# Retention layer of a hybrid decoder: chunks flow across heads, and PSUM banks are chosen by the expected end of their last use

## Chip, cores, metric

The kernel runs on the 8 cores of one Trainium2 chip. Each core has one prompt sequence of 2048 tokens (plus 16 meta tokens) and 16 of the 128 sample tokens; the cores share no data. The metric is device time of the slowest core, in microseconds. Some executions on all 8 cores are slower, with a lower granted clock on the cores of one die (one of the kernel before took 2028 us, with 0.83 on cores 0 to 3 and 0.96 on cores 4 to 7). They are called slow here; only the others, the fast ones, are compared.

## The reference, cut

Two layers: a pooling mixer with a SwiGLU feed-forward, then a retention mixer with a SwiGLU feed-forward. The change is in the retention mixer: four heads, keys of 256 and values of 512, in chunks of 128 tokens.

```python
def ret_chunk(q, k, v, s0, log_g):
    scores = jnp.einsum('bihd,bjhd->bhij', q, k) * dmask
    o = jnp.einsum('bhij,bjhe->bihe', scores, v)
    o = o + jnp.einsum('bihd,bhde->bihe', q, s0) * cross[None, :, :, None]
    s_new = gamma ** c * s0 + jnp.einsum('bjhd,bjhe->bhde', k * kdec, v)
    return o, s_new
# retention_mix: proj = xn @ w_in  -> q, k, v, gate; rotary on q and k; scan of ret_chunk over chunks;
# per-head group norm of o; (silu(gate) * o) @ w_out
```

The 2048 tokens are run as two halves of 1024. So there are two retention stages, each with 4 heads of 8 chunks, and between them lie the feed-forward layers and the sample tokens' states (here "the middle").

## The kernel before

One Python program emits the instructions of all engines, in an order that is fixed at build time. To choose it, the program keeps a clock of its own: every instruction has a modelled cost, and each engine a time at which it is free. Projections are emitted by plain loops. Work of the recurrence is in generators ("side tasks"), which are polled between blocks of a projection and go on when the modelled TensorE time has come to what they wait for. `drain` emits nothing else until a task is finished. A bank is a PSUM buffer of 128 x 512 numbers that a group of matmuls writes and another engine reads; five or six of them go round.

```python
        def bank(hold=False):
            sd.poll()
            ...
            while True:                      # round robin over the banks that nobody holds
                b = ring['b'][ring['i'] % len(ring['b'])]
                ring['i'] += 1
                if b not in held:
                    break
            if hold:
                held.append(b)
            return b
        ...
        def gate_gen(po, n, h, eps_ap, gdst, gsrc, after=None, guard=None, freed=None):
            yield after
            s, x = gn_stats(po, n, eps_ap)   # statistics: VectorE, GpSimd
            yield x
            o = on[onx[0] % 3]
            ...
            x = act(o[0:n, :], po, ACT.Identity, scale=s[0:n, 8:9], bias=s[0:n, 9:10])   # "on"
            if freed is not None:
                freed()                      # the bank may be given out again
            yield x
            yield from room(3)
            pt = bank(True)
            ...                              # four transposes of "on", four affine steps "af", product with the gate
        ...
        def a_gen(hf, h, gap):               # scores and decayed keys of a head, chunk by chunk
            ...
            for t in range(8):
                ps = bank()
                ...
                tt(PMt[:, t, :], ps[:, 0:128], causal, ALU.mult)
                act(KD[:, t, :], ptb, ACT.Copy, scale=float(gam[h] ** (-128.0 * t)))
                yield gap

        def b_gen(hf, h, gap):               # the recurrence
            q = Q[h % 2]
            So = FB[2]
            if hf == 0:
                ...
            else:
                load(So[:], sscr[h], ('fb', 2), ins=[('scr%d' % h)])
                acopy(psS[:], So[:].rearrange("p (c e) -> p c e", c=2))
            xs = acopy(Sbf[0][:], psS[:])
            ...
            for t in range(8):
                ...                          # 5 matmuls, cast of the state to Sbf, one gate_gen as its tail
            while any(x in sd.tasks for x in tails):
                yield 0.3

        def ret(hf, hh, qk_blocks, g_blocks, o_blocks, exit_fn):
            ...
            for h in range(4):
                qk_proj(hf, h, qk_blocks, h == 0)
                if h < 3:
                    g_proj(hf, h, g_blocks)
                sd.drain(bent)               # recurrence of the head before, with all its tails
                aent = sd.add(a_gen(hf, h, 1.3))
                v_proj(hf, h)
                sd.drain(aent)
                bent = sd.add(b_gen(hf, h, (1.5, 2.5, 2.5, 1.0)[h]))
                if h == 3:
                    g_proj(hf, h, g_blocks)
                if h:
                    ...
                    o_proj(hf, h - 1, hh, o_blocks)
            sd.drain(bent)
            ...
            o_proj(hf, 3, hh, o_blocks, exit_fn)
```

Scores `PMt`, decayed keys `KD`, values `V` and keys `K` have one buffer each; queries and gates have two. That is why the value projection of a head has to wait for the recurrence of the head before.

Of the kernel before, what the change touches and what calls it, by code (L numbers as in the profile page):

```python
# [54 lines left out]
class Prog:  # L55
# [109 lines left out]
    def _clock(self, o, ins, outs, cost, nbytes):  # L165

        t = self.free[o.eng]
        for d in o.deps:
            if d.is_dma or d.eng != o.eng:
                t = max(t, d.t + 0.12)  # L170
        if o.is_dma:
            busy = 1.1 if o.eng == 'pool' else 0.08
            self.free[o.eng] = t + busy
            self.dma_free = max(self.dma_free, t + busy) + nbytes / 330e3
            o.t = max(self.dma_free, t + busy + 2.0)
            return
        if cost is None:
            n = outs[0].free_size() if outs else 0
            if o.eng == 'act':
                cost = 0.22 + n / 1400.0  # L180
            elif o.eng == 'dve':
                cost = 0.08 + n / 960.0
            else:
                cost = 0.2 + n * 0.0024
        o.t = t + cost
        self.free[o.eng] = o.t
# [101 lines left out]
class Side:  # L288
# [33 lines left out]
    def drain(self, ent):  # L322
        while ent in self.tasks:
            nxt = min(e[0] for e in self.tasks)
            self.p.free['pe'] = max(self.p.free['pe'], nxt)
            self.poll()
# [26 lines left out]
def build_program():  # L353
# [40 lines left out]
    with st:  # L394
# [126 lines left out]
        held = []  # L521

        def room(k):
            while sum(b not in held for b in ring['b']) < k:
                yield 0.3

        def bank(hold=False):
            sd.poll()
            assert sum(b not in held for b in ring['b']) > 0
            while True:  # L530
                b = ring['b'][ring['i'] % len(ring['b'])]
                ring['i'] += 1
                if b not in held:
                    break
            if hold:
                held.append(b)
            return b
# [19 lines left out]
        def plan_ret():  # L557
            for h in range(4):
                wl.append(w_qk[h, 0])
                wl.append(w_qk[h, 1])  # L560
                for w in ((w_g, w_v) if h < 3 else (w_v, w_g)):
                    wl.append(w[h, 0])
                    wl.append(w[h, 1])
                if h:
                    wl.append(w_o[h - 1, 0])
                    wl.append(w_o[h - 1, 1])
            wl.append(w_o[3, 0])
            wl.append(w_o[3, 1])
# [120 lines left out]
        def pool_a(s0, T, special, ahead, pumps=()):  # L689
# [6 lines left out]
            def front(g):  # L696
                bd = B_BAND + g * 143
                DF = DFA[g % 2]
                for j in range(2):
                    c = 2 * g + j  # L700
                    pd = bank()
                    cc = slice(c * 128, (c + 1) * 128)
# [8 lines left out]
                    if special:  # L711
# [8 lines left out]
                        ts(DF[j][:, n + 16:n + 32], pp[:, 16:32], gcol, None, ALU.mult, ALU.bypass)  # L720
                    x = act(DF[j][:, 0:n], pd[:, 0:n], ACT.Copy, scale=gcol)
                pbs = []
                for m in range(2):
# [161 lines left out]
        stx = [0]  # L885
        gdone = {}
        afb = [False]

# [37 lines left out]
        def a_gen(hf, h, gap):  # L926
            q = Q[h % 2]
            yield rope[0]
            if hf == 0:
                pt = bank()  # L930
                ptb = pt[:].bitcast(BF16)[:, 0:256]
                for c in range(2):
                    tr(ptb[0:32, c * 128:(c + 1) * 128], K[:, c, 1024:1056], ident)
                acopy(KD[0:32, 8, :], ptb[0:32, :])
                copy(qS[:, h, :, :], q[:, :, 1024:1040], 'pool')
                copy(kS[:, h, :, :], K[:, :, 1024:1040], 'pool')
                yield gap
            for t in range(8):
                cc = slice(t * 128, (t + 1) * 128)
                ps = bank()  # L940
                for c in range(2):
                    mm(ps[:, 0:128], K[:, c, cc], q[:, c, cc], c == 0, c == 1)
                pt = bank()
                ptb = pt[:].bitcast(BF16)[:, 0:256]
                for c in range(2):
                    tr(ptb[:, c * 128:(c + 1) * 128], K[:, c, cc], ident)
                tt(PMt[:, t, :], ps[:, 0:128], causal, ALU.mult)
                act(KD[:, t, :], ptb, ACT.Copy, scale=float(gam[h] ** (-128.0 * t)))
                yield gap

        def b_gen(hf, h, gap):
            q = Q[h % 2]
            So = FB[2]
            if hf == 0:
                for c in range(2):
# [5 lines left out]
            yield xs  # L961
            tails = []
            for t in range(8):
                cc = slice(t * 128, (t + 1) * 128)
                while len(tails) > 2 and tails[-3] in sd.tasks:
                    yield 0.3
# [9 lines left out]
                else:  # L976
                    act(So[:].rearrange("p (c e) -> p c e", c=2), psS[:], ACT.Copy, scale=float(gam[h] ** 1024.0))
                    store((sscr if hf == 0 else nrp)[h], So[:], ('fb', 2), outs=[('scr%d' % h)] if hf == 0 else [])
                gs = G[h % 2][:, :, cc]
                tails.append(sd.add(gate_gen(psO[:], 128, h, cf[:, C_GE + h:C_GE + h + 1], gs, gs, after=xo,  # L980
                                             guard=lambda t=t: gdone[h] >= (t + 1) * 128, freed=lambda p=psO: held.remove(p))))
                yield xs
                yield gap
            while any(x in sd.tasks for x in tails):
                yield 0.3

# [39 lines left out]
        def v_proj(hf, h):  # L1026
            ws = [wget(), wget()]
            wv = [w[1][:].rearrange("p (k n) -> p k n", k=4) for w in ws]
            for t in ([8] if hf == 0 else []) + list(range(8)):
                n = 32 if t == 8 else 128  # L1030
                pb = bank()
                for k in range(8):
# [3 lines left out]
                if t == 8:  # L1036
                    acopy(vS[32 * h:32 * h + 16, :], pb[0:16, :])
                    store(vscr[:, h, :], vS[32 * h:32 * h + 16, :], 'vscr', outs=[('vscr%d' % h)])
                sd.poll()
# [20 lines left out]
        def o_proj(hf, h, hh, blocks, exit_fn=None):  # L1060
            ws = [wget(), wget()]
            wv = [w[1][:].rearrange("p (e n) -> p e n", e=4) for w in ws]

            def one(m, c0, n):
                pb = bank()
                for e in range(4):
# [129 lines left out]
        def ret(hf, hh, qk_blocks, g_blocks, o_blocks, exit_fn):  # L1196
            bent = None
            ring['b'] = psM + [psU] if hf == 0 else psM
            for h in range(4):
                gdone[h] = 0  # L1200
                qk_proj(hf, h, qk_blocks, h == 0)
                if h < 3:
                    g_proj(hf, h, g_blocks)
                sd.drain(bent)
                aent = sd.add(a_gen(hf, h, 1.3))
                v_proj(hf, h)
                sd.drain(aent)
                bent = sd.add(b_gen(hf, h, (1.5, 2.5, 2.5, 1.0)[h]))
                if h == 3:
                    g_proj(hf, h, g_blocks)  # L1210
                if h:
# [5 lines left out]
                    o_proj(hf, h - 1, hh, o_blocks)  # L1217
            sd.drain(bent)
            if hf == 1:
                copy(G[1][:, :, 1024:1040], gsm[:, 3, :, :], 'pool')  # L1220
            o_proj(hf, 3, hh, o_blocks, exit_fn)
            ring['b'] = psM

        def xload(h, xT, c0, n, k, eng='sp'):
# [190 lines left out]
```

## Time and profile before

| | us |
|---|---|
| device time, median of 3 | 1834.68 (1833.81 to 1837.03) |
| span of the slowest core (core 3) | 1829.8 |
| TensorE busy there | 1648.8, 90% |
| VectorE, ScalarE, GpSimd busy | 753, 695, 302 |

The stages of core 3 in the profile of the kernel before: first retention stage, middle, second retention stage. A stage here goes from its first query and key matmul to the first matmul of what follows, so it is 12 and 34 us wider than the windows that the prediction uses. After the times come length, busy us with instruction counts of PE (TensorE's matmuls), PEld (its weight loads), DVE (VectorE), ACT (ScalarE) and POOL (GpSimd), then TensorE's granted clock, the DMA share and GB/s. In the lists of waits further down, a line names the tile that waits, the engine and tile that it waits for, and then total us, number of waits and the longest.

```profile
325.18:667.63 342.45, 301.00 (x1817) 162.71 (x1814) 160.38 (x340) 170.92 (x336) 95.53 (x160) 0.97 0.36 73
667.63:1226.04 558.41, 515.88 (x2638) 237.21 (x2638) 234.68 (x328) 241.79 (x365) 55.91 (x95) 0.95 0.81 212
1226.04:1573.27 347.23, 295.48 (x1768) 161.82 (x1765) 169.20 (x375) 167.72 (x319) 95.25 (x152) 0.95 0.31 61
```

Length minus the first busy number is TensorE's idle time: 41 us, 43 us and 52 us. The busy number also holds the cost of a low clock, because a matmul at a lower clock is busy for longer (the prediction shows a group of eight that takes 3.59 us after a wait and 1.90 us elsewhere; the granted clock was 0.50 from 576 to 580 us and 1.00 from 360 to 364).

### The profile page before, as it was taken

The page shows a single profiled execution, that of the slowest core. Times are in us where ns is not written, and L with a number is a line of the kernel's source. Part 1 is how long each engine was busy: PE and PEld are TensorE (multiplying, and loading weights), DVE is VectorE, ACT ScalarE, POOL GpSimd, SP SyncE. Part 2 cuts the span into 40 slices and gives each one's busy share as a digit, 9 for nine tenths or more (in the row PEclk, how much of TensorE's full clock was granted, in tenths as well). Part 3 has the DMA queues.
Part 4 walks back from the last instruction along what each step waited for, and adds up shares of the span by engine and source line. Part 5 has one row for each costly group of instructions (what it writes and reads, how often), then busy time and mean ns, then how long its engine had stood idle before and what let it go on. Part 6 is the DMA issues. An engine that isn't in the chain of part 4 may idle for free.

```text
span 1829.8 us, 28085 instructions; the slowest of 8 cores (1811.3 to 1829.8 us)
## 1 busy us (share of the span) xinstructions
PE 1648.8 (90%) x9925; PEld 919.7 (50%) x9925; DVE 753.0 (41%) x1426; ACT 694.8 (38%) x1263; POOL 301.6 (16%) x505
## 2 busy tenths in 40 slices
PE   4999999898998888978997999999889976999997
PEld 3666666554544443433444444444454533666665
DVE  3532223442644463333346343353544625522224
ACT  3311112155545544433454444432545455310121
POOL 2010000341413111010011000022413312101000
PEclk9899999999998989988998999999999989999998
DMA  7357857623331349688779899772333232245432
GB/s 183 56 91 166 196 119 162 148 43 69 67 60 37 58 108 225 160 200 183 184 185 252 269 260 297 208 171 49 67 70 70 47 81 45 41 71 83 78 55 94
DMA packets 70680, 229.09 MB, mean 125 GB/s; under 512 B 7856, under 2 KB 11120, under 8 KB 70400
## 3 DMA queue, kind: packets, MB, share of 16 engines
q0 software_dynamic: 30224, 103.30, 32.9%
q1 hardware_dynamic: 40320, 124.00, 21.4%
q8 instruction: 83, 1.36, 0.3%
q14 instruction: 53, 0.43, 0.1%
HBM read 254.79 MB, written 62.00 MB: 173 GB/s over the span
## 4 chain that ended last, share of the span: by engine, by line
PE 76%; DVE 7%; DMA 6%; issue 4%; ACT 4%; POOL 2%; SPq 0%; DVEq 0%; POOLq 0%; ACTq 0%
PE pm L474 65%; PE psU L474 5%; PE psS L474 4%; DMA U<-xtok 4%; ACT on L491 2%; DVE xn L507 1%; DVE rot L498 1%; DVE stt L892 1%; ACT af L491 1%; PE pm L482 1%; DMA fb<-sret 1%; DMA U<-gb 1%; POOL U L498 1%; DMA U<-xsp 1%; POOL stt L626 1%
## 5 line engine op out<-in xcount | busy, mean ns | idle before, releaser
L474 PE MATMUL pm<-xn,w 128*128 128x512 bf16 (+7 forms) x4392 | 804.5, 342 | 34.2 <-DVE xn L507 12.9
L474 PEld LDWEIGHTS pm<-xn,w 128*128 128x128 bf16 x4392 | 431.2, 99 | 384.1 <-issue 65.8
L474 PE MATMUL pm<-U,w 128*128 128x512 bf16 (+4 forms) x2203 | 417.7, 346 | 25.1 <-ACT on L491 19.0
L474 PEld LDWEIGHTS pm<-U,w 128*128 128x128 bf16 x2203 | 215.7, 99 | 207.5 <-issue 42.4
L491 ACT ACTIVATE rot<-pm 128x512 bf16<-128x512 f32 (+4 forms) x202 | 104.7, 519 | 438.5 <-PE pm L474 438.5
L498 DVE TENSOR_TENSOR U<-pm,rot 128x512 bf16<-128x512 f32 (+4 forms) x187 | 112.4, 601 | 339.2 <-PE pm L474 331.0
L498 DVE TENSOR_TENSOR hB<-pm,hB 128x347 f32<-128x347 f32 (+2 forms) x161 | 87.1, 551 | 110.2 <-PE pm L474 107.8
L474 PE MATMUL pm<-w,xn 128*128 128x512 bf16 (+1 forms) x448 | 113.4, 399 | 0.0
L498 DVE TENSOR_TENSOR hA<-pm,hA 128x512 f32<-128x512 f32 (+2 forms) x121 | 76.6, 639 | 82.2 <-PE pm L474 82.1
L491 ACT ACTIVATE Sbf<-psS 128x1024 bf16<-128x1024 f32 x56 | 57.3, 1024 | 114.7 <-PE psS L474 114.7
L498 POOL TENSOR_TENSOR U<-rot 128x352 bf16<-128x352 f32 (+2 forms) x96 | 88.8, 946 | 71.9 <-DVE rot L498 71.8
L498 DVE TENSOR_TENSOR rot<-pm,cs_sb 128x352 f32<-128x352 f32 (+2 forms) x170 | 79.3, 512 | 31.0 <-PE pm L474 18.9
L491 ACT ACTIVATE U<-pm 128x256 bf16<-128x256 bf16 (+3 forms) x127 | 58.4, 461 | 84.2 <-PE pm L474 84.0
L491 ACT ACTIVATE af<-pm,cf_sb 128x128 f32<-128x128 bf16 x208 | 78.1, 462 | 21.0 <-PE pm L482 14.0
L498 DVE TENSOR_TENSOR U<-af,U 128x512 bf16<-128x512 f32 x64 | 52.5, 821 | 75.6 <-ACT af L491 75.6
L200 POOL DMA_DIRECT2D w<-w_gu x71 | 40.4, 570 | 257.9 <-PE pm L474 203.9
L491 ACT ACTIVATE U<-pm,cf_sb 128x512 bf16<-128x512 f32 (+1 forms) x72 | 49.0, 686 | 76.7 <-PE pm L474 76.7
L498 DVE TENSOR_TENSOR U<-pm,cb_sb 128x128 bf16<-128x128 f32 x64 | 18.7, 292 | 136.6 <-PE pm L482 101.2
L200 POOL DMA_DIRECT2D w<-w_d x48 | 26.8, 559 | 271.3 <-PE pm L474 230.8
L626 POOL TENSOR_TENSOR stt<-stt,cf_sb 128x1 f32<-128x1 f32 x65 | 39.0, 600 | 172.3 <-DVE stt L502 166.5
L491 ACT ACTIVATE xn<-hB 128x512 bf16<-128x512 f32 (+2 forms) x80 | 42.3, 544 | 66.2 <-DVE hB L498 66.0
L474 PEld LDWEIGHTS pm<-w,xn 128*128 128x128 bf16 (+1 forms) x448 | 42.7, 101 | 45.4 <-issue 8.4
(214 smaller groups left out, 1502.8 us busy)
## 6 DMA issues: line engine op xcount, KB each, us to landing
w<-w_gu POOLq DMA_DIRECT2D x71, 512.0 KB, 7.2
fb<-sret SPq DMA_DIRECT2D x36, 512.0 KB, 7.7
nrs<-fb SPq DMA_DIRECT2D x36, 512.0 KB, 7.2
w<-w_d POOLq DMA_DIRECT2D x48, 352.0 KB, 5.3
hA<-sret SPq DMA_DIRECT2D x28, 512.0 KB, 6.7
nrs<-hA SPq DMA_DIRECT2D x28, 512.0 KB, 5.4
c_gu<-w SPq DMA_DIRECT2D x17, 512.0 KB, 6.6
w<-c_gu POOLq DMA_DIRECT2D x17, 512.0 KB, 9.2
```

Of the source, the lines that this page charges most:

```text
L200: h.dma_start(out=o_ap, in_=i_ap).then_inc(s, 16)
L474: return P.op('pe', lambda h: h.matmul(out, lhsT=lhsT, rhs=rhs, start=start, stop=stop, skip_group_check=skip), ins=[lhsT, rhs], outs=[out ...
L482: return P.op('pe', lambda h: h.transpose(out, in_, idn), ins=[in_, idn], outs=[out], cost=0.056)
L491: return P.op('act', lambda h: h.activation(out=out, in_=in_, func=func, scale=scale, **kw), ins=ins, outs=[out] + ([accum] if accum is no ...
L498: return P.op(eng, lambda h: h.tensor_tensor(out=out, in0=a, in1=b, op=op), ins=[a, b], outs=[out])
L507: return P.op('dve', lambda h: h.scalar_tensor_tensor(out=out, in0=a, scalar=s, in1=b, op0=op0, op1=op1), ins=ins, outs=[out])
L626: return P.op('pool', lambda h: h.tensor_tensor(out=dst, in0=dst, in1=cf[0:n, C_NH:C_NH + k], op=ALU.pow), ins=[dst, cf[0:n, C_NH:C_NH + k ...
L892: P.op('dve', lambda h: h.bn_stats(out=s[0:n, 0:6], in_=po), ins=[po], outs=[s[0:n, 0:6]])
```

## The change

Its intent: the drain between heads goes. Each chunk waits only for the chunk whose buffer it takes, so the recurrence of one head runs on through the projections of the next. A bank is given out by the modelled end of its last use. The modelled costs of ScalarE and VectorE are made a little higher.

```diff
@@ the program's clock
             if o.eng == 'act':
-                cost = 0.22 + n / 1400.0
+                cost = 0.32 + n / 1450.0
             elif o.eng == 'dve':
-                cost = 0.08 + n / 960.0
+                cost = 0.13 + n / 1000.0
@@ banks
+        def idle_since(b):
+            k = P._keys(b[:])[0][0]
+            st = P.segs.get(k)
+            assert st is None or st[0].eng != 'pe' or not st[1]
+            return max(st[0].t if st else 0.0, P.free['pe']), taken.get(k, 0)
+
         def bank(hold=False):
             sd.poll()
-            ... round robin ...
+            b = min((x for x in ring['b'] if x not in held), key=idle_since)
+            ring['i'] += 1
+            taken[P._keys(b[:])[0][0]] = ring['i']
@@ a_gen (the bank of the scores is now held until the mask is applied; so is one in the pooling front)
+                while h and prog['b', h - 1] < t + 1:
+                    yield 0.3
-                ps = bank()
+                yield from room(2)
+                ps = bank(True)
@@ b_gen
+            while prog['v', h] < 1 or prog['a', h] < 1 or h and prog['b', h - 1] < 8:
+                yield 0.3
-                while len(tails) > 2 and tails[-3] in sd.tasks:
+                while len(tl) > 2 and tl[-3] in sd.tasks or prog['v', h] < t + 1 or prog['a', h] < t + 1:
                     yield 0.3
-            while any(x in sd.tasks for x in tails):
-                yield 0.3
@@ v_proj
+                if h:
+                    sd.until(lambda: prog['b', h - 1] > t % 8)
@@ o_proj, before each block
+                for t in range(8):
+                    if t * 128 < c0 + n:
+                        sd.until(lambda: len(tails[h]) > t and tails[h][t] not in sd.tasks)
@@ ret
                 qk_proj(hf, h, qk_blocks, h == 0)
-                if h < 3:
-                    g_proj(hf, h, g_blocks)
-                sd.drain(bent)
                 aent = sd.add(a_gen(hf, h, 1.3))
+                g_proj(hf, h, g_blocks)
+                sd.add(b_gen(hf, h, GAPS[h]))          # GAPS = (2.5, 2.5, 2.5, 1.0)
                 v_proj(hf, h)
                 sd.drain(aent)
-                bent = sd.add(b_gen(hf, h, (1.5, 2.5, 2.5, 1.0)[h]))
-                if h == 3:
-                    g_proj(hf, h, g_blocks)
...
-            sd.drain(bent)
```

Cut: the updates of the counters `prog`, and the weights' order for the last head, which follows the program.

More of the change, by code (lines that the diff above doesn't have):

```diff
@@ L322, in drain, with until @@
     def drain(self, ent):
-        while ent in self.tasks:
+        self.until(lambda: ent not in self.tasks)
+    def until(self, cond):
+        while not cond():
             nxt = min(e[0] for e in self.tasks)
@@ L525, in room @@
                 yield 0.3
+        taken = {}
+        def idle_since(b):
[3 more added lines that the diff above has]
+            return max(st[0].t if st else 0.0, P.free['pe']), taken.get(k, 0)
         def bank(hold=False):
             sd.poll()
-            assert sum(b not in held for b in ring['b']) > 0
-            while True:
-                b = ring['b'][ring['i'] % len(ring['b'])]
-                ring['i'] += 1
-                if b not in held:
-                    break
+            b = min((x for x in ring['b'] if x not in held), key=idle_since)
+            ring['i'] += 1
+            taken[P._keys(b[:])[0][0]] = ring['i']
             if hold:
@@ L560, in plan_ret @@
                 wl.append(w_qk[h, 1])
-                for w in ((w_g, w_v) if h < 3 else (w_v, w_g)):
+                for w in (w_g, w_v):
                     wl.append(w[h, 0])
@@ L700, in front @@
                     c = 2 * g + j
-                    pd = bank()
+                    pd = bank(True)
                     cc = slice(c * 128, (c + 1) * 128)
@@ L721, in front @@
                     x = act(DF[j][:, 0:n], pd[:, 0:n], ACT.Copy, scale=gcol)
+                    held.remove(pd)
                 pbs = []
@@ L886, in build_program @@
         gdone = {}
+        prog = {}
+        tails = {}
         afb = [False]
@@ L928, in a_gen @@
             yield rope[0]
+            while h and prog['b', h - 1] < 1:
+                yield 0.3
             if hf == 0:
@@ L947, in a_gen @@
                 tt(PMt[:, t, :], ps[:, 0:128], causal, ALU.mult)
+                held.remove(ps)
                 act(KD[:, t, :], ptb, ACT.Copy, scale=float(gam[h] ** (-128.0 * t)))
+                prog['a', h] = t + 1
                 yield gap
@@ L953, in b_gen @@
             So = FB[2]
+            while prog['v', h] < 1 or prog['a', h] < 1 or h and prog['b', h - 1] < 8:
+                yield 0.3
             if hf == 0:
@@ L961, in b_gen @@
             yield xs
-            tails = []
+            tl = tails[h] = []
             for t in range(8):
                 cc = slice(t * 128, (t + 1) * 128)
-                while len(tails) > 2 and tails[-3] in sd.tasks:
+                while len(tl) > 2 and tl[-3] in sd.tasks or prog['v', h] < t + 1 or prog['a', h] < t + 1:
                     yield 0.3
@@ L979, in b_gen @@
                 gs = G[h % 2][:, :, cc]
-                tails.append(sd.add(gate_gen(psO[:], 128, h, cf[:, C_GE + h:C_GE + h + 1], gs, gs, after=xo,
+                tl.append(sd.add(gate_gen(psO[:], 128, h, cf[:, C_GE + h:C_GE + h + 1], gs, gs, after=xo,
                                              guard=lambda t=t: gdone[h] >= (t + 1) * 128, freed=lambda p=psO: held.remove(p))))
+                prog['b', h] = t + 1
                 yield xs
                 yield gap
-            while any(x in sd.tasks for x in tails):
-                yield 0.3
         rope = [None]
@@ L1037, in v_proj @@
                     acopy(vS[32 * h:32 * h + 16, :], pb[0:16, :])
+                else:
+                    prog['v', h] = t + 1
+                if t == 8:
                     store(vscr[:, h, :], vS[32 * h:32 * h + 16, :], 'vscr', outs=[('vscr%d' % h)])
@@ L1196, in ret @@
         def ret(hf, hh, qk_blocks, g_blocks, o_blocks, exit_fn):
-            bent = None
             ring['b'] = psM + [psU] if hf == 0 else psM
             for h in range(4):
-                gdone[h] = 0
+                gdone[h] = prog['a', h] = prog['b', h] = prog['v', h] = 0
+            for h in range(4):
                 qk_proj(hf, h, qk_blocks, h == 0)
-                if h < 3:
-                    g_proj(hf, h, g_blocks)
-                sd.drain(bent)
                 aent = sd.add(a_gen(hf, h, 1.3))
+                g_proj(hf, h, g_blocks)
+                sd.add(b_gen(hf, h, GAPS[h]))
                 v_proj(hf, h)
                 sd.drain(aent)
-                bent = sd.add(b_gen(hf, h, (1.5, 2.5, 2.5, 1.0)[h]))
-                if h == 3:
-                    g_proj(hf, h, g_blocks)
                 if h:
@@ L1222, in ret @@
             ring['b'] = psM
+        GAPS = (2.5, 2.5, 2.5, 1.0)
         def xload(h, xT, c0, n, k, eng='sp'):
```

## The prediction

> **What bounds the kernel now.** I read the page first: TensorE is busy for 90% of the span, no other engine above 41%, so time comes only from TensorE's idle time and from a slow clock.
>
> ```profile
> PE 1648.8 (90%) x9925; PEld 919.7 (50%) x9925; DVE 753.0 (41%) x1426; ACT 694.8 (38%) x1263; POOL 301.6 (16%) x505
> ...
> PE   4999999898998888978997999999889976999997
> ...
> PEclk9899999999998989988998999999999989999998
> ```
>
> The idle time is 1829.8 - 1648.8 = 181.0 us. The row of tenths dips in three places: the start, the middle, and the two retention stages. Next I read the busy time by stage, to place the change. The columns are PE, PEld, DVE, ACT, POOL, clock, DMA share, GB/s.
>
> ```profile
> 150.00:200.00 50.00, 50.00 (x337) 32.78 (x336) 14.61 (x28) 2.78 (x6) 5.00 (x10) 1.00 0.75 155
> ...
> 325.00:655.00 330.00, 289.87 (x1734) 157.01 (x1733) 150.20 (x324) 164.06 (x325) 93.52 (x158) 0.96 0.36 72
> ...
> 1243.00:1556.00 313.00, 266.93 (x1573) 143.92 (x1572) 142.16 (x319) 158.10 (x298) 87.03 (x142) 0.97 0.32 63
> ```
>
> A feed-forward stretch is full (50.00 of 50.00 at clock 1.00); nothing can be won there. The two retention stages leave 40.1 and 46.1 us of TensorE idle, 86.2 us together. ScalarE is only half busy in them (164.06 of 330). Third view: TensorE's waits in the first, then in the second retention stage.
>
> ```profile
> PE pm L474 <- ACT on L491: 14.7, 12, 2.5
> PE pm L482 <- ACT on L491: 12.9, 6, 4.4
> PE pm L474 <- DVE xn L507: 4.7, 1, 4.7
> PE pm L474 <- ACT af L491: 3.7, 4, 1.8
> PE psU L474 <- ACT on L491: 2.0, 1, 2.0
> PE psU L474 <- ACT af L491: 1.0, 1, 1.0
> ```
>
> ```profile
> PE pm L482 <- ACT on L491: 23.2, 12, 4.0
> PE pm L474 <- ACT on L491: 15.9, 8, 2.4
> PE pm L474 <- ACT Sbf L491: 2.9, 4, 1.4
> PE psU L474 <- ACT on L491: 1.9, 1, 1.9
> PE psU L482 <- ACT on L491: 1.5, 1, 1.5
> ```
>
> L474 is the matmul helper and L482 the transpose helper; "on" is the group-normalised output of a chunk. So two kinds of waits carry the loss. Kind A: a projection's matmul waits although its data is old. What it waits for is the bank it was given, which ScalarE is still reading (on, af). First stage 14.7 + 3.7 + 2.0 + 1.0 = 21.4; second 15.9 + 1.9 = 17.8; together **39.2 us in 27 waits**. Kind B: the transposes of "on" come before their input is there. 12.9 + 23.2 + 1.5 = **37.6 us in 19 waits**. Kind C, the cast state Sbf: 0.8 + 2.9 = **3.7 us**. The timeline of TensorE shows both of the first two:
>
> ```profile
> 534.86 1.89 PE L474 MATMUL pm<-U,w 128*128 128x512 bf16 x8
> 538.32 1.02 PE L474 MATMUL pm<-U,w 128*128 128x512 bf16 x4 [1.57 <-ACT on L491]
> ```
>
> ```profile
> 568.20 0.59 PE L474 MATMUL psS<-U 128*128 128x512 bf16 x2
> 573.20 0.59 PE L482 MATMUL pm<-cb_sb,on 128*128 128x128 bf16 x4 [4.40 <-ACT on L491]
> 575.63 0.59 PE L482 MATMUL pm<-cb_sb,on 128*128 128x128 bf16 x4 [1.84 <-ACT on L491]
> 576.14 3.59 PE L474 MATMUL pm<-w,xn 128*32 128x512 bf16 x8
> ```
>
> The first is kind A inside the output projection. The second is the drain at the end of a head: the last chunk's normalisation runs alone, and only then does the value projection (576.14) start. It needed nothing of that head but room in the value, score and key buffers.
>
> [...] at 573.20 one transpose holds back a projection whose inputs are ready. [...] after the 4.40 us wait, eight matmuls of 512 columns take 3.59 us; the same group takes 1.90 us at 362.13. [...] The kernel does rotate; kind A shows that a blind rotation meets long holders. [...]
>
> **The change part by part.** No arithmetic is added or removed: the same matmuls, casts and transfers. What moves is the order fixed at build time, by a clock that the program models.
>
> *Bank choice.* Round robin gives way to the bank with the earliest expected end of its last use. The model's ScalarE cost goes from 0.22 + n/1400 to 0.32 + n/1450: 0.59 to 0.67 at 512, 0.95 to 1.03 at 1024, against 0.69 and 1.02 in the trace, so these expectations are good. One gap stays: the model prices the statistics by their 6 outputs, 0.14 us against 0.69 measured, so it thinks "on" ready some 0.6 us early. There are five or six banks, and a chunk holds one or two of them, so another bank is nearly always free earlier. I take 80% of kind A: 0.8 x 39.2 = **31 us**.
>
> *Waits per chunk.* The drain ahead of each value projection goes. Scores of head h run beside its gate projection, its recurrence beside its value projection, the previous head's output projection, and the next head's query and key projections. Would the recurrence be done when the next head needs its buffers? A chunk costs five matmuls of 0.215 = 1.07 us, then the cast 1.02 and its hops, then the gap of 2.5: about 5 us, 40 us for eight. The value projection is 8 x 1.73 = 14 us, the output projection 16 x 0.86 = 14, query and key 14, plus the chunks' own 8.6: about 50 us. So the new waits are met before they are reached. Only the last head cannot hide all: its final chunk's chain (statistics 0.69 + 0.18 + 0.21, GpSimd 0.56 + 0.26, ScalarE 0.78, transposes, four af 1.50, product 0.69, hops) is some 6 us, but the output projection's first block of 8 x 0.86 = 7 us needs only early chunks. I take 80% of kind B: 0.8 x 37.6 = **30 us**; and 70% of C: **2.6 us**.
>
> *Clock.* I compared slow groups after the waits with normal ones. At 426 1.5 us are lost, at 576 2.0, at 648 2.1 (16 matmuls in 5.75 for about 3.6), at 1328 1.7, at 1406 1.5, at 1472 to 1481 2.5, at 1530 1.5: 12.8 us. With the waits of 3 us and more gone, most returns: **10 us**.
>
> *New cost.* In the last head all per-chunk work meets: value copy 0.69, key copy 0.38, Sbf 1.02, on 0.78, af 1.50: 4.4 us of ScalarE per chunk, against 1.73 + 0.43 + 1.07 + 0.22 = 3.5 us of TensorE. I allow 2 us per stage there, 2 per stage for transposes put too early (before, waits of 0.45 to 1.3 us apart from drains), and 1 per stage for the end: **10 us**. Banks held in the pooling front and longer holds of scores cost nothing that I can see.
>
> Sum: 31 + 30 + 2.6 + 10 - 10 = 63.6 us. 1834.7 - 63.6 = **1771 us**, 3.5% less.
>
> **The rivals.** *ScalarE becomes the bound.* The new overlap puts casts, value copies and affine steps in the same 20 us. For it: 4.4 against 3.5 us per chunk. Against: only the last head has the short gap of 1.0; the others start a chunk about every 5 us, and the output projection beside it gives ScalarE nothing. If it holds in every head, 4 us in each of eight heads come back: about 1800 us. *The waits move.* Bank waits become early-transpose waits, as the hidden 0.6 us comes up for each of 64 chunks. For it: seven or so such waits exist already. Against: projection blocks of 0.6 to 1.7 us between polls usually cover it. If half of the chunks pay 0.6: 19 us, so about 1785. *The gain meets something outside.* The middle, with 11.0 us on pooling input, might absorb an earlier start. But its work is placed relative to TensorE's progress, so I expect it to move along whole; 5 us either way.
>
> **Range and chances.** If bank choice and chunk flow recover 95% and the new cost is 4: 37 + 36 + 3 + 12 - 4 = 84, so about 1750. If they recover 55% with half of the clock and 12 lost: 22 + 21 + 2 + 6 - 12 = 39, so about 1796. I give **1748 to 1801**. The 2% line is 1798, near that upper end: faster 0.86, same 0.12, slower 0.02.
>
> **What would show it.** Right: in the retention stages TensorE's idle falls from 86 to about 25 us, "pm L474 <- ACT on" to below 8, no transposes wait over 3 us outside a last head, and the clock there is near 0.99. Wrong: waits on value copies (U from pm) or on score reads appear, ScalarE near 90% in the value projections (first rival); transposes with more waits than 19 and a sum above 20 us (second); or shorter retention stages with a longer middle (third).

## The result, and the profile after

| | before | after |
|---|---|---|
| device time, median of 4 runs each | 1834.24 us | 1752.10 us (1747.89 to 1753.17) |
| ratio of fast runs | | 0.9546 (95%: 0.9526 to 0.9566) |

A ratio is the mean time of one kernel's fast runs over that of the other's fast runs of the same rounds, so it is not quite the ratio of the medians. The change saves 82 us where 63.6 were predicted; 1752 lies in the predicted range, near its lower end. Results are correct.

The page of the kernel after (slowest core: core 1). The matmul helper is now L477, the transpose helper L485.

```profile
PE 1627.1 (93%) x9925; PEld 913.3 (52%) x9925; DVE 749.2 (43%) x1426; ACT 693.7 (40%) x1263; POOL 302.6 (17%) x505
...
PE   4999999999999989897997999999989998999997
...
PEclk7899999999999999998998999999999999999998
```

The instruction counts are the same as before: 9925 matmuls, 1426 on VectorE, 1263 on ScalarE. Only order and banks moved. The same three stages, on core 1:

```profile
323.61:637.08 313.47, 295.90 (x1816) 162.59 (x1814) 163.29 (x346) 171.70 (x337) 97.89 (x160) 0.98 0.41 79
637.08:1182.99 545.91, 508.95 (x2638) 233.65 (x2638) 232.67 (x325) 240.67 (x364) 54.20 (x94) 0.97 0.82 216
1182.99:1499.37 316.38, 288.91 (x1768) 160.76 (x1766) 164.62 (x375) 166.19 (x318) 95.49 (x153) 0.96 0.34 66
```

The retention stages are 29 and 31 us shorter. Their idle time falls from 41 to 18 and from 52 to 27 us, and their busy time by 5 and 7 us at a higher clock (0.97 to 0.98 and 0.95 to 0.96). TensorE's waits in the first, then in the second retention stage after:

```profile
PE psU L477 <- ACT on L494: 5.3, 7, 1.2
PE pm L477 <- DVE U L501: 3.4, 4, 2.0
PE pm L477 <- DVE xn L510: 3.1, 3, 2.1
PE pm L477 <- ACT xn L494: 2.1, 2, 1.8
PE psU L485 <- ACT on L494: 0.6, 1, 0.6
```

```profile
PE pm L477 <- DVE U L501: 6.9, 5, 4.1
PE pm L477 <- ACT U L494: 6.1, 1, 6.1
PE pm L477 <- ACT on L494: 5.5, 5, 1.3
PE pm L477 <- DVE xn L510: 4.0, 7, 2.0
PE pm L485 <- ACT on L494: 3.0, 4, 1.1
```

The long waits of transposes on "on", up to 4.4 us, are gone: none is above 1.1. Bank waits on "on" are left, but none is above 1.3. New are a single wait of 6.1 us on ScalarE's value copy (`U`) and waits on VectorE's `U` of up to 4.1. The experiments come back to both.

### The profile page after: what moved, and what is told of

It reads as the page before. It is cut to its first block, busy times and chain, and to the rows that moved or that the text cites. A ratio compares the mean times of both kernels' runs of the same rounds, so it can differ in the third digit from the quotient of the medians.

```text
span 1751.4 us, 28088 instructions; the slowest of 8 cores (1741.4 to 1751.4 us)
## 1 busy us (share of the span) xinstructions
PE 1627.1 (93%) x9925; PEld 913.3 (52%) x9925; DVE 749.2 (43%) x1426; ACT 693.7 (40%) x1263; POOL 302.6 (17%) x505
## 4 chain that ended last, share of the span: by engine, by line
PE 77%; DMA 8%; DVE 7%; issue 3%; ACT 2%; POOL 2%; SPq 0%; DVEq 0%; POOLq 0%; ACTq 0%
PE pm L477 65%; PE psU L477 6%; DMA U<-xtok 5%; PE psS L477 5%; DVE xn L510 1%; PE pm L485 1%; ACT on L494 1%; DMA nrs<-fb 1%; DVE stt L904 1%; DVE hB L501 1%; DMA fb<-sret 1%; DVE rot L501 1%; DVE hA L501 1%; DMA U<-xsp 1%; POOL stt L635 1%
## 5 line engine op out<-in xcount | busy, mean ns | idle before, releaser
L477 PE MATMUL pm<-xn,w 128*128 128x512 bf16 (+7 forms) x4368 | 798.2, 340 | 19.6 <-DVE hA L510 9.4
L477 PEld LDWEIGHTS pm<-xn,w 128*128 128x128 bf16 x4368 | 426.2, 99 | 357.6 <-issue 42.7
L477 PE MATMUL pm<-U,w 128*128 128x512 bf16 (+4 forms) x2173 | 407.9, 344 | 14.0 <-DVE U L501 7.8
L477 PEld LDWEIGHTS pm<-U,w 128*128 128x128 bf16 x2173 | 211.4, 98 | 190.0 <-issue 22.7
L501 DVE TENSOR_TENSOR hB<-pm,hB 128x346 f32<-128x346 f32 (+2 forms) x154 | 83.4, 552 | 104.1 <-PE pm L477 103.5
L477 PE MATMUL pm<-w,xn 128*128 128x512 bf16 (+1 forms) x480 | 112.7, 383 | 7.1 <-ACT U L494 6.1
L501 POOL TENSOR_TENSOR U<-rot 128x352 bf16<-128x352 f32 (+2 forms) x96 | 90.3, 962 | 58.4 <-DVE rot L501 58.3
L494 ACT ACTIVATE U<-pm 128x256 bf16<-128x256 bf16 (+3 forms) x124 | 54.1, 460 | 73.3 <-PE pm L477 73.1
L635 POOL TENSOR_TENSOR stt<-stt,cf_sb 128x1 f32<-128x1 f32 x65 | 39.2, 604 | 246.2 <-DVE stt L505 246.2
L477 PEld LDWEIGHTS pm<-w,xn 128*128 128x128 bf16 (+1 forms) x480 | 45.5, 98 | 59.9 <-issue 11.2
```

Of the source, the lines that this page charges most:

```text
L477: return P.op('pe', lambda h: h.matmul(out, lhsT=lhsT, rhs=rhs, start=start, stop=stop, skip_group_check=skip), ins=[lhsT, rhs], outs=[out ...
L494: return P.op('act', lambda h: h.activation(out=out, in_=in_, func=func, scale=scale, **kw), ins=ins, outs=[out] + ([accum] if accum is no ...
L501: return P.op(eng, lambda h: h.tensor_tensor(out=out, in0=a, in1=b, op=op), ins=[a, b], outs=[out])
L635: return P.op('pool', lambda h: h.tensor_tensor(out=dst, in0=dst, in1=cf[0:n, C_NH:C_NH + k], op=ALU.pow), ins=[dst, cf[0:n, C_NH:C_NH + k ...
```

## The experiments

Most of what follows is read from two tables. Each number is the mean over all 8 cores of the profiled execution, which is steadier than one core. First the length of the stages, in us. "Start" is all before the first query and key matmul, "end" all after the second retention stage.

| kernel | start | retention 1 | middle | retention 2 | end | ratio to before |
|---|---|---|---|---|---|---|
| before | 321.9 | 343.0 | 551.4 | 347.5 | 256.6 | 1 |
| before, again | 324.0 | 343.1 | 553.0 | 347.5 | 257.0 | |
| costs only | 325.6 | 340.9 | 555.7 | 357.1 | 253.9 | 1.0063 |
| bank choice only | 320.8 | 328.6 | 545.8 | 334.9 | 251.2 | 0.9837 |
| bank choice, costs | 322.5 | 325.6 | 547.2 | 342.8 | 253.0 | 0.9835 |
| flow only | 323.3 | 337.2 | 546.5 | 334.2 | 259.1 | 0.9866 |
| flow, costs | 326.9 | 333.9 | 541.2 | 327.7 | 254.1 | 0.9814 |
| bank choice, flow | 321.9 | 317.5 | 543.8 | 316.8 | 251.8 | 0.9620 |
| after (all three) | 323.4 | 313.3 | 540.0 | 317.8 | 252.5 | 0.9546 |
| after, again | 322.3 | 313.5 | 537.6 | 317.2 | 252.3 | 0.9549 |

Second, TensorE's waits in the two retention stages together. Kind A are matmuls that wait for ScalarE's "on" or "af" to free their bank; kind B are transposes that wait for "on".

| kernel | A, bank waits | B, early transposes | A + B |
|---|---|---|---|
| before | 39.5 | 37.7 | 77.2 |
| costs only | 44.5 | 42.4 | 86.9 |
| bank choice only | 16.3 | 42.0 | 58.3 |
| bank choice, costs | 3.6 | 56.6 | 60.2 |
| flow only | 51.9 | 11.4 | 63.3 |
| flow, costs | 51.7 | 1.9 | 53.6 |
| bank choice, flow | 26.9 | 3.5 | 30.4 |
| after | 11.0 | 4.0 | 15.0 |

### The parts one by one

The change has three parts: the bank choice, the flow of chunks, and the modelled costs. The theory of the prediction is that bank choice and flow remove separate waits, so their gains add. The rivals are that waits only change their kind, and that the costs do part of the work. "Flow" takes several edits together: the waits per chunk, the new place of the last head's gate projection and the longer gap of the first head. Both single parts carry the two longer holds. These were not tried apart, but for the last head's drain at the end. Four kernels:

```diff
 # bank choice only: the kernel before with
+            b = min((x for x in ring['b'] if x not in held), key=idle_since)     # as in the change, with both longer holds
 # costs only: the kernel before with
+                cost = 0.32 + n / 1450.0      # ScalarE; VectorE 0.13 + n / 1000.0
 # flow only: the kernel after with
-            b = min(...); cost = 0.32 + n / 1450.0; cost = 0.13 + n / 1000.0
+            ... round robin ...; cost = 0.22 + n / 1400.0; cost = 0.08 + n / 960.0
 # bank choice and flow: the kernel after with
-                cost = 0.32 + n / 1450.0; cost = 0.13 + n / 1000.0
+                cost = 0.22 + n / 1400.0; cost = 0.08 + n / 960.0
```

> Only the bank choice (with the two longer holds it needs), old order of work, old modelled costs. Theory of the prediction: bank waits of kind A (39.2 us in the kernel before) fall by about 80%, the transposes' waits (37.6 us) stay: 31 us plus some clock, time near 1798, retention stages about 15 us shorter each, the middle unchanged. Rival 'the waits move': the transposes' waits grow by what the bank waits lose, time above 1820. Second rival, that the bank choice also carries the 11 us found in the middle: middle shorter by about 11 us and time near 1788.

Measured: ratio 0.9837 (0.9797 to 0.9878), mean of its four fast runs 1799.8 us. Kind A falls from 39.5 to 16.3, kind B stays and even grows a little, from 37.7 to 42.0. The theory holds for this part. The second retention stage of the slowest core (core 2):

```profile
PE pm L482 <- ACT on L491: 25.8, 14, 4.0
PE pm L474 <- ACT on L491: 3.8, 4, 1.6
PE psU L482 <- ACT on L491: 3.7, 2, 2.9
```

The transposes at the drains (L482, up to 4.0 us each) are untouched; the matmuls' bank waits on "on" (L474) are down to 3.8 us, from 17.8 in the prediction's window of this stage (core 3).

> Only the new modelled costs of ScalarE and VectorE, all else as before. Theory of the prediction: nearly nothing, within 10 us of 1834. Rival: better timed polls carry the gain found outside the retention stages (about 11 us in the middle and 5 at the end), time near 1818, retention stages unchanged.

Measured: ratio 1.0063 (1.0029 to 1.0098): slightly slower, by the second retention stage (357 us against 347). The rival falls; the costs alone win next to nothing (2 to 3 us in the first retention stage and at the end). The theory allowed within 10 us of 1834; the fast runs' mean is 1845.6, 11 to 12 above.

> Only the new order of the retention stage with its waits per chunk (round robin banks with the longer holds of the changed kernel, old modelled costs). Theory of the prediction: the transposes' waits fall by about 30 us and the clock returns some 8 us, bank waits of kind A stay near 39 us: time near 1797. Rival: with ScalarE busier beside the value projections, bank waits under round robin grow to 55 us or more, and the time stays above 1815, so that the flow pays only with the bank choice.

Measured: ratio 0.9866 (0.9835 to 0.9898), fast runs' mean 1809.5 us. Kind B falls from 37.7 to 11.4, as the theory has it, but kind A grows from 39.5 to 51.9, as the rival has it. The time lies between the two. The second retention stage of its slowest core (core 2) shows the new mix:

```profile
PE pm L477 <- ACT on L494: 12.2, 9, 3.5
PE pm L477 <- ACT af L494: 10.1, 10, 2.3
PE pm L485 <- ACT on L494: 6.4, 8, 1.5
```

Without drains, more chunks' "on" and "af" lie in ScalarE's queue while projections take banks in turn, and round robin hands out banks that are still in that queue.

> Bank choice and new order, but the old modelled costs, that is the changed kernel without its new costs. Theory of the prediction: within 10 us of the changed kernel's 1752. Rival: the expected ends of use are too early by 0.1 us per ScalarE instruction, waits of transposes and banks come back by 20 us, and the middle loses its 11 us: near 1780.

Measured: ratio 0.9620 (0.9569 to 0.9670). Two of its four runs were slow; the fast ones took 1760.8 and 1767.6 us, 12 us above 1752 in the mean, a little outside the theory's 10. The costs are worth about 0.7% on top (0.9546 against 0.9620, from different calls, intervals nearly touching). The waits say where: kind A is 26.9 us without the new costs and 11.0 with them, as the choice reads the modelled ends. The loss that the rival expects in the middle is not there beyond 4 us.

The gains do not add: 0.9837 x 0.9866 = 0.9705 for bank choice and flow, if they were separate; measured together, 0.9620. In the waits, bank choice alone takes away 77.2 - 58.3 = 18.9 us, flow alone 13.9, both 46.8.

The two cells that were left, bank choice with costs and flow with costs, ran later:

> Bank choice and new modelled costs, old order with its drains: the missing cell. Theory (the costs serve the bank choice, which reads them): bank waits on normalised chunks fall from the 16 us of the bank choice alone to about 8, the transposes' waits stay near 42 us as the drains stay; retention stages 660 us together against 664 with the bank choice alone; time near 1797. Rival (the costs help only the flow): bank waits stay at 16 us or more.

Measured: ratio 0.9835 (0.9815 to 0.9856), as with the bank choice without the costs, but this time is not clean. In the profiled execution cores 0 to 5 had a mean granted clock of 0.942 to 0.950, cores 6 and 7 of 0.960 and 0.958; here core 0, with 0.81, and then core 6, which was spared, from 660 to 800 us of the middle:

```profile
660.00:800.00 140.00, 138.66 (x562) 59.17 (x572) 53.93 (x79) 56.14 (x86) 13.44 (x25) 0.81 0.80 186
```

```profile
660.00:800.00 140.00, 131.61 (x626) 60.58 (x638) 57.27 (x84) 57.12 (x89) 14.92 (x27) 0.98 0.84 199
```

In its other two fast executions the slowest core, too, has a low mean clock (0.947 and 0.945). So the times don't settle whether the costs gain or lose here; the retention stages do, as the stretch shown lies outside them (the first ends at 648 us in the mean). They are 668.4 us together (667.4 on the two spared cores), against 663.5 with the bank choice alone and about 660 expected. Kind A did fall, to 3.6 us, but kind B grew to 56.6 where the theory had it stay near 42: what the banks gave, the transposes took. The second retention stage of core 2:

```profile
PE pm L482 <- ACT on L491: 33.2, 16, 4.0
PE psU L482 <- ACT on L491: 4.9, 4, 2.6
```

One bank wait on "on" is left in this stage, of 0.2 us, and the stage is longer than with the bank choice alone (342.8 against 334.9, in the mean). So with the drains in place the better timed bank choice only moves waits: A + B is 60.2 us, against 58.3 with the bank choice alone.

> The new order and the new modelled costs, banks in round robin: the last cell. Theory (the costs do nothing without a bank choice that reads them): bank waits stay near 52 us, time within 10 us of the flow alone, 1800 to 1820, retention stages 671 us together within 6. Rival (the costs alone mend the timing of the flow): bank waits below 40, time under 1795.

Measured: ratio 0.9814 (0.9786 to 0.9842). Bank waits 51.7 us, as the theory says: without a choice that reads them, the costs do not touch kind A. But they do bring kind B from 11.4 to 1.9 us and the retention stages to 661.6 us, below the 671 within 6 that the theory named. So the costs also time the transposes of the flow better. The time, 1796 us in the median, lies just below the theory's 1800 to 1820 and just above the rival's 1795.

### The unchanged kernels again, for the middle

The middle was 11 us shorter after, and the prediction had put no gain there.

> The changed kernel once more, so that the next three have it on the same chip, and for the spread of the middle between two traces of one kernel. Retention stages again 313 and 318 us (mean over cores). If the 11 us gained in the middle belong to the change, the middle is 540 within 3 us; if the middle is only wherever the transfers land, it moves by 5 us or more without any edit.

Measured: 1751.8 us, ratio 0.9549; retention stages 313.5 and 317.2; middle 537.6.

> The kernel before, unchanged, for a second trace of it. The changed kernel and its three near relatives have a middle of 536 to 541 us (mean over cores, five traces), the kernel before had 551 in its one. If the gain in the middle is the change's, this trace has 548 to 555 again and the ends of 256 to 257; if it was chance of the transfers, it comes below 545.

Measured in one execution: middle 553.0, end 257.0. In this trace cores 4 and 5 had a mean granted clock of 0.948 and 0.947, the others 0.955 to 0.966; without these two the middle is 550.6. So the shorter middle belongs to the change: 551 in two traces before, 540 and 537.6 in two after. The table does not give it to one part: bank choice alone 545.8, flow alone 546.5, both 543.8; with the costs as well, 541.2 for the flow and 539.0 for the bank choice (its two spared cores), and the costs alone 555.7. Cores of one trace differ by 10 us and more (544.8 us on core 1 and 558.4 on core 3 of the first trace before). The middle is the same work as before, but its side tasks (sample states, pooling of the second half) are placed by the same clock and take their banks by the same rule; which placement gains is open. The end, 4 us shorter, goes with the bank choice in the main: 251 to 253 in every kernel with it, 254 to 259 without. The costs alone bring it from 256.6 to 253.9.

### The 6 us wait on the value copy

A wait on ScalarE's value copy was what the prediction named as a sign of its first rival, a full ScalarE. The timeline of the kernel after, core 1, says something else:

```profile
1285.02 0.33 SPq L200 DMA_DIRECT2D fb<-sscr  x1
1288.36 1.02 ACT L498 COPY psS<-fb 128x1024 f32<-128x1024 f32 x1 [7.18 <-DMA fb<-sscr]
1289.47 1.01 ACT L498 CAST Sbf<-psS 128x1024 bf16<-128x1024 f32 x1
1290.38 1.27 ACT L494 ACTIVATE U<-pm,cf_sb 128x512 bf16<-128x512 f32 x2
...
1291.22 3.14 PE L477 MATMUL pm<-w,xn 128*128 128x512 bf16 x7 [6.09 <-ACT U L494]
```

ScalarE idles for 7.18 us. Next in its program is the copy of the head's saved state (`fb<-sscr`), whose load is issued only at 1285.02, because the state of the head before has to be stored from the same buffer first (issued at 1281.29). The value copies behind it wait: TensorE had written their input by 1285.1 (16 matmuls from 1281.51, 3.62 us), but ScalarE ran none of them in its 7.18 us, and the first starts at 1290.38. All banks fill, and TensorE stops for 6.09 us. Before, the same load was issued while the value projection ran, and the copy stood behind all its value copies in ScalarE's order, beside output or query and key projections, whose banks VectorE empties. On core 3 the copy then starts 18 us after the load, without a wait:

```profile
1328.58 0.33 SPq L200 DMA_DIRECT2D fb<-sscr  x1
...
1346.76 1.03 ACT L495 COPY psS<-fb 128x1024 f32<-128x1024 f32 x1
```

Also tested: what is left of kind A.

```diff
 # state loaded early: the kernel after with
-            So = FB[2]
+            So = FB[2] if hf == 0 else FB[(h + 2) % 3]
-                load(So[:], sscr[h], ('fb', 2), ins=[('scr%d' % h)])
@@ ret, at the head's start
+                if hf == 1:
+                    if h == 1:
+                        sd.drain(samp['ent'])
+                    i = (h + 2) % 3
+                    load(FB[i][:], sscr[h], ('fb', i), ins=[('scr%d' % h)])
 ...                                     # cut: the store of the state follows its buffer
 # statistics priced: the kernel after with
-            P.op('dve', ... bn_stats ...)
+            P.op('dve', ... bn_stats ..., cost=0.13 + 512 / 1000.0)
```

> The changed kernel with the state of each head of the second sequence half loaded at the head's start into a buffer of its own, no longer just before its use into the buffer that the head before still has to store. Theory (the 6 us that TensorE waited for ScalarE's value copies in the second retention stage are a transfer that ScalarE's copy of the state waits for, at the head of its queue): the wait of matmuls on value copies, 6.2 us, disappears, second retention stage 318 to about 310 with the clock, first unchanged, ratio to the changed kernel about 0.996. Rival (ScalarE is simply full there): the wait stays at 4 us or more and moves to another copy.

Measured: ratio 0.9481 (0.9457 to 0.9505), 1740.5 us; against the kernel after on the same chip, 0.9481 / 0.9549 = 0.993. The second retention stage goes from 317.2 to 304.2 us, the first stays at 313.7. Its three largest waits in the profile (core 0):

```profile
PE pm L477 <- ACT on L494: 5.6, 5, 1.4
PE pm L477 <- DVE xn L510: 3.9, 7, 2.0
PE pm L477 <- DVE U L501: 3.1, 4, 1.9
```

The wait on the value copy is gone, and nothing of its size took its place (bank waits of this stage in the mean 5.5 to 6.8). The gain of 13 us is more than the 6.3: 3.8 us of waits on VectorE's products went too, as the order after it shifted, and 5.4 us of busy time with the clock (0.96 to 0.98). ScalarE was not full. This kernel beats both the kernel before and the change.

> The changed kernel with the statistics instruction priced at 0.64 us in the program's clock where it had 0.14 (the trace shows 0.69). Theory (the 11 us of bank waits on the normalised chunks that are left, 0.7 and 1.05 us each, come of banks expected back some 0.6 us too early): matmuls on normalised chunks fall from 11 to below 4 us, transposes from 4 to below 2, retention stages 4 us shorter each. Rival (no bank is free there at all): the bank waits stay at 9 us or more, only the transposes gain.

Measured: ratio 0.9535 (0.9514 to 0.9555), so nothing clear of noise. Bank waits go from 11.0 to 6.6 us: in the second stage from 5.5 to 1.7, in the first only from 5.5 to 4.9. Transposes wait 3.3 us, not below 2. The second stage is 312.6 us long, 4.6 less than in the kernel after, the first 313.1; neither theory nor rival holds whole. The mispriced statistics explain the second stage's bank waits; the 0.7 us waits of the first, nearly all on one bank (psU in the listing further up), are not explained.

> Both edits. If the two are separate causes the gains add: about 15 us less than the changed kernel, near 1737. If not, one gain.

Measured: ratio 0.9480 (0.9460 to 0.9500), median 1740.6, the same as with the early load alone. No second gain is shown.

### The last head's drain

```diff
 # the kernel after with
+            sd.until(lambda: len(tails[3]) == 8 and not any(x in sd.tasks for x in tails[3]))
             o_proj(hf, 3, hh, o_blocks, exit_fn)
```

> The changed kernel with the last head's drain put back ahead of its output projection, for the size of that one part. Theory of the prediction: the drain cost 3.8 and 3.1 us of waits and some 3 us of slow clock before, and the waits per block that took its place cost 2.0 and 5.9 us (1 per stage was allowed): so the drain costs at most 5 us in the two stages together, ratio to the changed kernel 1.000 to 1.003. Rival (the flow into the last projection is where the change gains): both stages grow by 5 us or more each, ratio 1.006 and up.

Measured: ratio 0.9595 (0.9578 to 0.9612), against the kernel after 0.9595 / 0.9549 = 1.005 (on two chips): between the two theories' numbers. But the retention stages did not grow: 312.3 and 317.4 us, against 313.5 and 317.2 for the kernel after. Kind B grows from 4.0 to 13.9 us, and what it replaces is the waits of the last output projection on the gated product. In the kernel after, core 1, that is

```profile
1479.65 1.32 PE L477 MATMUL pm<-U,w 128*128 128x347 bf16 x4 [1.82 <-DVE U L501]
...
1490.87 1.31 PE L477 MATMUL pm<-U,w 128*128 128x346 bf16 x4 [4.05 <-DVE U L501]
```

and 1.97 us in the first stage: 7.8 us. So the flow into the last projection won nothing; one wait took the place of another. The slower time comes from the middle. In the profiled run cores 2, 3, 6 and 7 had a granted clock of 0.81 in every 20 us from 660 to 780 us. Core 2 and then core 0 from 660 to 780 us:

```profile
660.00:780.00 120.00, 120.00 (x499) 51.09 (x498) 43.66 (x64) 46.38 (x71) 11.46 (x22) 0.81 0.81 193
```

```profile
660.00:780.00 120.00, 112.48 (x551) 52.06 (x559) 46.88 (x69) 47.43 (x74) 12.07 (x22) 1.00 0.88 220
```

Core 2 is busy all the time and shows 499 matmuls, core 0 shows 551 with 7.5 us of idling. The four undisturbed cores have a middle of 533 us, shorter than the kernel after. In the other three runs two or more cores also have a mean clock of 0.952 to 0.958, where the kernel after has at least 0.964. The edit is not needed for it: on the same chip the unchanged kernel before had a low mean clock on cores 4 and 5 (0.948 and 0.947), and the bank choice with costs on cores 0 to 5 (0.942 to 0.950). Whether the edit makes it more frequent, these runs do not settle. The spared cores end at 1727 to 1740 us, so the 1.005 is no cost of the drain that these runs show.

## Why the prediction was right, point by point

All by the means over the cores, for the two retention stages together. The stage windows are wider than the prediction's, so the waits before are 39.5, 37.7 and 3.7 us in place of its 39.2, 37.6 and 3.7.

| term | predicted us | measured us |
|---|---|---|
| kind A, bank waits | -31 | 39.5 to 11.0: -28.5 |
| kind B, early transposes | -30 | 37.7 to 4.0: -33.7 |
| kind C, Sbf | -2.6 | 3.7 to 0: -3.7 |
| clock (busy time) | -10 | 596.3 to 585.4: -10.9 |
| other and new waits | +10 | 11.6 to 27.6: +16.0 |
| retention stages, sum | -63.6 | 690.5 to 631.1: -59.4 |
| start, middle, end | 0, 5 either way | +1.5 - 11.4 - 4.1 = -14.0 |

The terms sum to -60.8 and the stages to -59.4, because idle time counted from waits and from lengths differs by 1.3 us (rounding is the rest). From the sum to the 82 us: 59.4 in the stages, 14.0 outside them, 5.0 from the slowest core (below), and some 4 because the profiled execution of the kernel before (1831.3 us) was faster than the median.

- **The bound and the two kinds of waits: right.** The parts alone remove the kinds that they were said to remove: the bank choice A, the flow B. In windows cut as the prediction cut its own (324 to 624.5 and 1199 to 1482 us, core 1) TensorE's idle time is 35 us, from 86, where about 25 was forecast; the clock there is 0.99 and 0.98, as forecast.
- **The sizes of A, B, C and the clock: right** within 4 us each.
- **The new cost: mis-sized, 10 against 16.** Of the three parts of that term, early transposes were put at 4 us, on top of the 7.5 of kind B that were to stay; all of kind B is 4.0, and the table has it in row B. So like with like the miss is larger, 6 against 16. The end of the last head was put at 1 per stage and is 7.8 in all. "ScalarE becomes the bound" was given 2 per stage; what came was 6.2 us in one place, and the early load shows that it was a transfer ahead in ScalarE's queue, not ScalarE's load. No rival named it.
- **Outside: the step that missed.** "I expect it to move along whole; 5 us either way": the middle became 11.4 us shorter in the mean, again so in a second trace of both kernels, and the end 4.1. This term, 14 us, is most of the distance between 1771 and 1752. A further 5 us is the slowest core: it stood 9.4 us above the mean before (1829.8 against 1820.4) and 4.4 after (1751.4 against 1747.0), and the time is the slowest core's.
- **"The waits move": put aside too lightly.** It does not hold for the whole change, but each part alone meets it. Flow alone raises A by 12 us; bank choice with the right costs raises B by 19. The prediction's sum treats A and B as separate, and it came out right only because both were treated at once. The range needed no luck from outside: the stages' 59.4 us alone would have given about 1775.
- **The clock:** of the 12.8 us that I counted in slow groups, 9.8 stand after stretches whose longest wait was 2.96 to 4.40 us, the other 3.0 after waits of 1.94 and 2.34; that 10 us would return was an estimate from these, and 10.9 did. The feed-forward stretch that I read had a clock of 1.00 (50.00 us busy of 50.00). Later traces show 0.81 on some cores in the middle (core 2 of the run with the last drain from 660 to 780 us, 120.00 us busy of 120.00).
- **A small slip that changes nothing:** 1771 + 19 is 1790, where the second rival says 1785.

## What to carry to other kernels

When an engine loses time to short waits on buffers and to drains, look at both before valuing either: here the two cures gave 1.6% and 1.3% alone and 3.8% together, because each wait that went let the engine run into the other kind. A choice by expected time is as good as the times that it reads; of the 26.9 us of bank waits that bank choice and flow leave, 15.9 went with less than a tenth of a microsecond more of modelled cost per instruction. After moving work to a new neighbour, look at what stands ahead of it in the same queue: one late load in front of the value copies cost more (6.2 us) than all early transposes (4.0).

## What the traces show beside the change

- The low clock took some cores of a die and not others: 0.81 on cores 2, 3, 6 and 7 while core 0, of the same die as 2 and 3, had 1.00 (660 to 780 us of the run with the last drain). Later in that run, from 1000 to 1120 us, all 8 cores had 1.00, with TensorE busy for 19.79 us or more of every 20.
- The order of the banks matters when holders differ: choosing the bank with the earliest expected release, with two longer holds and nothing else changed, took bank waits from 39.5 to 16.3 us.
- The batch-norm statistics took 0.69 us for 128x512 from PSUM, their aggregation 0.18 us (kernel before, core 3).
